# Output columns 1024 to 2047 with a fourth pair by seven products, and written orders for the sums, the passage and the end

## The chip, the cores and the metric

The kernel runs on one core of one Trainium2 chip. The metric is the device time in microseconds of one execution. A core has TensorE (PE in the profile, with PEld for its loads of weights), VectorE (DVE), ScalarE (ACT), GpSimd (POOL) and SyncE (SP), which issues nearly all transfers here. Each engine takes its own queue of instructions in order and waits at an instruction until what it needs is there.

## The reference

One layer of a gated short convolution with modulation by a vector c, for 256 tokens, D = 2048 and E = 4096:

```python
h = rmsnorm(x, norm_g)
mod = silu(c) @ ada_w + ada_b
shift, scale, gate = split(mod, 3)
h = h * (1 + scale) + shift
b_gate, c_gate, v, g = split(h @ w_in, 4)          # 2048 -> 4 * 4096
u = causal_depthwise_conv(c_gate * v, conv_w)      # width 3
y = b_gate * u * silu(g)
out = rmsnorm(x + gate * (y @ w_out), final_g)     # 4096 -> 2048
```

All is float32. The kernel splits each float32 factor of the large products into a rounded high part and a low part, and adds three products: high by high, low by high, high by low.

## The kernel before

**Up to the output product.** The input product (L491) and all that stands ahead of it fill the first 727 us; the diff leaves them as they are but for one instruction on ACT near their end. The result y lies as 16 pairs of row blocks (`ys[0]` to `ys[15]`, each 256 rows of E by 256 tokens, in high and low parts).

**The output product** runs in two halves of 1024 output columns, both by `columns`. Each step n takes one pair j from a written order: it loads 256 rows of `w_out` by 1024 columns (1 MB, `load_o`, L711), ACT makes the high part by a cast (`split_hi`, L352), DVE the low part by a subtraction (`split_lo`, L357), and PE multiplies (`triple`, L722): for 2 tiles of 128 tokens, 2 row blocks and 2 groups of 512 columns, 3 matmuls each, so 24 matmuls of 512 columns.

Pairs in `sevens` go through `seven` instead: a 2 by 2 block product by seven products in place of eight, with sums of blocks of y (`forms`, made earlier for pairs 10 to 15) and of the weights. That is 21 matmuls. DVE makes the sums of the weights (L742, L744, L745) and the low part of the weights as they are (1536 wide, L746), ACT their high part (1536 wide, L743), and then the sums are split like a normal pair's piece (2048 wide, L352 and L357). When the last of the `sevens` is through, `gather` (L764, L765) brings their shared sums into `ends`.

**Buffers.** Loaded weights and sums of weights take turns in three buffers of the kind "lo"; a load is issued once DVE has done with the piece that lay there three turns before. High parts take turns in three buffers of the kind "hi", low parts in three of "raw"; these come free when PE is through with the piece of three turns before.

**The passage between the halves.** When the first half is done, DVE adds its banks to `ends`, applies the gate, adds x and weights by `final_g` (`gated`, L730 to L733), and ACT takes the squares, while PE runs the first pairs of the second half.

**The end.** Columns 1024 to 1535 (the third quarter) and 1536 to 2047 (the fourth) end apart. In the second half's `columns` the fourth quarter gets pairs 0 to 5 and 10 to 15, and so does the third. The pieces of `LAST` (ep 3 and 4, pairs 6 to 9) then come for the third quarter alone. The fourth quarter's sums so far are gated, x is added (L847 to L849), and ACT copies them into the banks `po[0]` and `po[1]` (L850), one per tile of tokens t. The weights of the last pieces are multiplied by the gate on DVE (L862), split, and PE adds them straight onto `po[t]`: 24 matmuls for t = 0, 24 for t = 1. The root of the norm (L818, which needs ACT's table of roots), the scaling (`finish`, L824 to L828) and the stores (L829) close each t.

**What sets the order.** A scheduler places each engine's instructions by a simulated timeline; `tc.add_manual_dep` with `after` keeps one instruction behind another on its engine without any signal, `in_order` does so for all instructions of a block, and `later` lowers a block's priority.

Of the kernel before, what the change touches and what calls it, by code (L numbers as in the profile page):

```python
# [13 lines left out]
P = 128  # L14
D = 2048
# [102 lines left out]
def short_conv_layer(ctx: ExitStack, tc: tile.TileContext, x, c, norm_g, ada_w, ada_b, w_in, conv_w, w_out, final_g, out):  # L118
# [224 lines left out]

    def hi_tile():
        return w_tile("hi", "hi", F32R)
# [9 lines left out]
    def split_lo(raw, n, hi, lo_tag="lo", lo=None):  # L355
        lo = lo_tile(lo_tag) if lo is None else lo
        nc.vector.tensor_tensor(out=lo[:, :n], in0=raw[:, :n], in1=hi[:, :n].bitcast(F32), op=ALU.subtract)  # L357
        return hi, lo
# [271 lines left out]
    forms = {}  # L630

# [22 lines left out]
    for ct in range(NS, NCT, 2):  # L654
        for q in QUARTERS:
# [25 lines left out]
            elif q == 3:  # L681
                nc.scalar.activation(z, bank, AF.Silu)
# [23 lines left out]

    fsq = const.tile([P, TT, 3], F32, tag="fsq", name="fsq")
# [16 lines left out]
    def gated(t, c0, n, src, pr, at):  # L724


        cs = slice(c0, c0 + n)
        r = xr[:, t, cs]
        g = gates[c0 // 1024].rearrange("p a f -> p (a f)")[:, c0 % 1024 : c0 % 1024 + n]
        nc.vector.tensor_tensor(out=pr, in0=src, in1=g, op=ALU.mult)  # L730
        nc.vector.tensor_tensor(out=r, in0=r, in1=pr, op=ALU.add)
        nc.scalar.activation(pr, r, AF.Square, scale=D**-0.5, accum_out=fsq[:, t, at : at + 1])
        nc.vector.tensor_tensor(out=r, in0=r, in1=fg[:, cs], op=ALU.mult)  # L733


    def seven(j, raw, bank, p1, p6, p75, opens, last):
# [5 lines left out]
        nc.vector.tensor_tensor(out=s[:, 0:2], in0=b[:, 1:3], in1=b[:, 0:1].to_broadcast([P, 2, W]), op=ALU.subtract)  # L742
# [67 lines left out]
    for t in range(TT):  # L810
        c = ends[t].rearrange("p h f -> p (h f)")
        with later(350):
            gated(t, 0, 2 * W, c, c, 0)

    def finish(t):
# [20 lines left out]
        2 * W, (0, 1, 2, 10, 3, 13, 11, 4, 14, 12, 5, 15), SEVEN[0:3],  # L836
# [8 lines left out]
    for t in range(TT):  # L845
        c = ends[t][:, 1]
        nc.vector.tensor_tensor(out=c, in0=halves[1][:, t], in1=c, op=ALU.add)  # L847
        nc.vector.tensor_tensor(out=c, in0=c, in1=gate(3), op=ALU.mult)
        nc.vector.tensor_tensor(out=c, in0=c, in1=xr[:, t, 3 * W : 4 * W], op=ALU.add)  # L849
        nc.scalar.copy(po[t], c)  # L850
# [6 lines left out]
    late = []  # L857
    for ep in LAST:
# [4 lines left out]
        hi, lo = split(raw, SLOT, "raw")  # L863
        out_mm(po[0], 0, ep, hi, lo)
        late.append((ep, hi, lo))
    for t in range(TT):
        c = ends[t][:, 0]
        nc.vector.tensor_tensor(out=c, in0=halves[0][:, t], in1=c, op=ALU.add)
        gated(t, 2 * W, W, c, c, 1)
# [3 lines left out]
    for t in range(TT):  # L873
        if t == 1:
            for ep, hi, lo in late:
                out_mm(po[1], 1, ep, hi, lo)
        nc.scalar.activation(ends[t][:, 1], po[t], AF.Square, scale=D**-0.5, accum_out=fsq[:, t, 2:3])
        finish(t)
# [24 lines left out]
```

## Time and profile before

| | us |
|---|---|
| median of 3 runs (lowest, highest) | 905.64 (905.23, 906.0) |
| the profiled execution's own time | 905.34 |
| its span, first to last instruction | 903.6 |
| PE, output product begins | 726.73 |
| PE, second half begins | 809.92 |
| DMA, mean share of its 16 engines in the last 24 us | 0.25 |

The page gives for each engine its busy time; a timeline row gives start, length, engine, line, what is written from what, and in brackets how long the engine stood idle ahead of it and what released it. A matmul's length in the timeline is longer than the distance to the next, since matmuls overlap. In a row of chain or waits "PE mm L722 <- ACT mm L850" reads: the matmuls of line 722 into an `mm_1` bank waited for ACT's write into it at line 850. The two banks named `mm_1` serve the sevens as `p1` and `p6` and afterwards as `po[0]` and `po[1]`.

### The profile page before, as it was taken

To read this page: it belongs to the slowest core of one execution; us is meant where nothing else is said; L and a number is where in the kernel's file an instruction comes from. 1 tells how busy PE (TensorE), PEld (TensorE's weight loads), DVE (VectorE), ACT (ScalarE), POOL (GpSimd) and SP (SyncE) were. 2 spreads that over 40 slices of the span, in tenths; PEclk is the share of its full clock that TensorE was granted. 3 is DMA by queue.
4 is the path that set the end of the run, shared out by engine and by line. 5 is a ranking of instruction groups with operands and counts; after the bars stand their busy time and mean duration, and the time that the engine had idled before them with its cause. 6 is when DMAs were issued, how large, how long until landed. Compare 5 with 4: busy or idle time off the path is not lost.

```text
span 903.6 us, 16403 instructions
## 1 busy us (share of the span) xinstructions
PE 888.2 (98%) x7000; PEld 851.0 (94%) x7000; DVE 670.2 (74%) x661; ACT 482.4 (53%) x427; POOL 87.3 (10%) x95
## 2 busy tenths in 40 slices
PE   7999999999999999999999999999999999999996
PEld 4899999999999999999999999999999988888884
DVE  5889989888888867765875677565555578889685
ACT  6767866665548756644433434443434435544443
POOL 0000000000000132024324303320000000000000
PEclk9999999999999999999999999999999999999999
DMA  9999999999998587687988888866666486675652
GB/s 309 366 368 368 363 313 354 353 369 351 351 328 286 162 279 247 187 257 236 287 238 241 257 279 263 248 211 200 188 187 190 138 304 209 212 251 163 214 182 94
DMA packets 159594, 235.01 MB, mean 260 GB/s; under 512 B 6804, under 2 KB 105284, under 8 KB 159136
## 3 DMA queue, kind: packets, MB, share of 16 engines
q1 hardware_dynamic: 156384, 226.56, 76.7%
q0 software_dynamic: 3008, 7.34, 2.8%
q8 instruction: 55, 0.90, 0.4%
q14 instruction: 19, 0.16, 0.1%
q10 hardware_dynamic: 128, 0.04, 0.0%
HBM read 224.49 MB, written 2.10 MB: 251 GB/s over the span
## 4 chain that ended last, share of the span: by engine, by line
PE 90%; DMA 4%; DVE 2%; ACT 1%; SPq 1%; issue 1%; ACTq 0%
PE mm_b L491 39%; PE mm_s L491 36%; PE mm_w L722 7%; PE mm_o L722 5%; PE mm L722 4%; DMA at<-in_ada_w_dram 2%; DVE lo L357 1%; SPq L231 1%; DMA raw_s<-in_sc_w_in_dram 1%; ACT hi L352 1%; DMA x<-in_x_dram 1%; DMA raw_o<-in_sc_w_out_dram 1%; PE tp_g L481 0%; DVE raw_o L862 0%; ACT mm_s L524 0%
## 5 line engine op out<-in xcount | busy, mean ns | idle before, releaser
L491 PE MATMUL mm_s<-hT,hi 128*128 128x256 f32 x2048 | 350.3, 277 | 1.8 <-ACT hT L328 1.0
L491 PE MATMUL mm_b<-hT,hi 128*128 128x256 f32 x2048 | 348.2, 276 | 0.0
L491 PEld LDWEIGHTS mm_s<-hT,hi 128*128 128x128 f32 x2048 | 308.1, 188 | 2.4 <-ACT hT L328 1.2
L491 PEld LDWEIGHTS mm_b<-hT,hi 128*128 128x128 f32 x2048 | 308.6, 188 | 0.0
L491 PE MATMUL mm_b<-hT,lo 128*128 128x256 f32 x1024 | 282.6, 276 | 0.0
L491 PE MATMUL mm_s<-hT,lo 128*128 128x256 f32 x1024 | 282.0, 277 | 0.1
L357 DVE TENSOR_TENSOR lo<-raw,hi 128x2048 fp32r<-128x2048 f32 (+1 forms) x66 | 151.8, 2301 | 101.4 <-ACT hi L352 101.1
L352 ACT CAST hi<-raw 128x2048 fp32r<-128x2048 f32 (+1 forms) x66 | 123.7, 1875 | 191.6 <-PE mm_b L491 150.7
L491 PEld LDWEIGHTS mm_b<-hT,lo 128*128 128x128 f32 x1024 | 192.2, 188 | 0.0
L491 PEld LDWEIGHTS mm_s<-hT,lo 128*128 128x128 f32 x1024 | 191.7, 188 | 0.3 <-DVE lo L357 0.3
L357 DVE TENSOR_TENSOR lo<-raw_s,hi 128x2048 fp32r<-128x2048 f32 (+1 forms) x80 | 149.3, 1872 | 39.6 <-ACT hi L352 39.1
L352 ACT CAST hi<-raw_s 128x2048 fp32r<-128x2048 f32 (+1 forms) x80 | 123.9, 1557 | 56.1 <-PE mm_s L491 51.7
L474 DVE SCALAR_TENSOR_TENSOR gv<-at,silu_c,gv 128x512 f32<-128x512 f32 x105 | 78.6, 749 | 3.6 <-DMA at<-in_ada_w_dram 1.9
L512 ACT COPY acc<-mm_s 128x1024 f32<-128x1024 f32 x54 | 54.7, 1013 | 42.4 <-PE mm_s L491 42.3
L357 DVE TENSOR_TENSOR lo<-raw_o,hi 128x2048 fp32r<-128x2048 f32 x23 | 52.5, 2289 | 25.7 <-ACT hi L352 25.7
L352 ACT CAST hi<-raw_o 128x2048 fp32r<-128x2048 f32 x23 | 43.8, 1908 | 48.4 <-PE mm_o L722 17.3
L722 PE MATMUL mm_o<-hi,y 128*128 128x512 f32 x188 | 59.0, 389 | 0.0
L722 PE MATMUL mm_w<-hi,y 128*128 128x512 f32 x184 | 58.8, 389 | 0.0
L623 POOL TENSOR_TENSOR gacc<-gacc,z 128x512 f32<-128x512 f32 x28 | 45.9, 1639 | 119.3 <-DMA z<-gacc 119.3
L617 DVE SCALAR_TENSOR_TENSOR gacc<-at_g,silu_c,gacc 128x512 f32<-128x512 f32 x60 | 45.9, 764 | 8.0 <-DMA at_g<-in_ada_w_dram 6.9
L621 POOL DMA_DIRECT2D z<-gacc x28 | 15.7, 561 | 330.6 <-DVE acc L558 284.9
L722 PEld LDWEIGHTS mm_o<-hi,y 128*128 128x128 f32 x188 | 35.3, 188 | 7.3
(152 smaller groups left out, 675.4 us busy)
## 6 DMA issues: line engine op xcount, KB each, us to landing
raw<-in_sc_w_in_dram SPq DMA_DIRECT2D x64, 1024.0 KB, 5.8
raw_s<-in_sc_w_in_dram SPq DMA_DIRECT2D x47, 1024.0 KB, 7.7
raw_o<-in_sc_w_out_dram SPq DMA_DIRECT2D x32, 1024.0 KB, 5.2
at<-in_ada_w_dram SPq DMA_DIRECT2D x114, 256.0 KB, 7.8
raw_s<-in_sc_w_in_dram SPq DMA_DIRECT2D x33, 512.0 KB, 6.7
at_g<-in_ada_w_dram SPq DMA_DIRECT2D x32, 512.0 KB, 7.8
at<-in_ada_w_dram SPq DMA_DIRECT2D x6, 512.0 KB, 9.3
x<-in_x_dram SPq DMA_DIRECT2D x4, 512.0 KB, 6.2
```

Of the source, the lines that this page charges most:

```text
L231: nc.sync.dma_start(at[:, :, s, :], adas[:, j : j + kk, s, 0 : NK0 * P])
L352: nc.scalar.copy(hi[:, :n], raw[:, :n])
L357: nc.vector.tensor_tensor(out=lo[:, :n], in0=raw[:, :n], in1=hi[:, :n].bitcast(F32), op=ALU.subtract)
L474: nc.vector.scalar_tensor_tensor(out=gv, in0=at4[:, i], scalar=c_k, in1=gv, op0=ALU.mult, op1=ALU.add)
L491: mm = last_mm[0] = nc.tensor.matmul(dst, w, h[k], start=begins and left, stop=ends, skip_group_check=True)
L512: nc.scalar.copy(acc[ch, q], bank)
L617: nc.vector.scalar_tensor_tensor(out=ga, in0=at3[:, i, :], scalar=s, in1=ga, op0=ALU.mult, op1=ALU.add)
L621: nc.gpsimd.dma_start(turned[0 : P - away], ga[away:P])
L623: nc.gpsimd.tensor_tensor(out=ga, in0=ga, in1=turned, op=ALU.add)
L722: nc.tensor.matmul(dst, y[a], b, start=opens and i == 0, stop=ends and i == 2, skip_group_check=True)
```

## The change

- The second half's order of pairs becomes 0, 1, 2, 10, 3, 11, 4, 12, 5, 13, 14, 15, and its `sevens` are 10 to 13 in place of 10 to 12.
- In `seven` the first sum of the weights stays behind the last low part that was traced before it.
- `gated` is divided into `residual` and `weighted`; its operations stay the same.
- The passage of the fourth quarter into `po` (`move`), the gate product of the last pieces (`gated_piece`) and everything behind them stand in one `in_order` block: piece 3, then the three sums and the copy of t = 0, then piece 4, then those of t = 1; `finish(0)` is traced ahead of `po[1]`'s matmuls, and t = 1's third quarter is weighted behind `finish(0)`.
- A root of a constant (`warm2`) is taken behind the last SiLU, so that ACT's table of roots is loaded there.

```diff
+    last_silu = ended_silu[0]
+    warm2 = const.tile([P, 1], F32, tag="fs", name="warm2", bufs=2)
+    early = nc.scalar.activation(warm2, eps_t, AF.Sqrt)
+    tc.add_manual_dep(early.ins, last_silu.ins.name, after, reason="the table of roots is there at the end")
...
-        nc.vector.tensor_tensor(out=s[:, 0:2], in0=b[:, 1:3], in1=b[:, 0:1].to_broadcast([P, 2, W]), op=ALU.subtract)
+        first = nc.vector.tensor_tensor(
+            out=s[:, 0:2], in0=b[:, 1:3], in1=b[:, 0:1].to_broadcast([P, 2, W]), op=ALU.subtract
+        )
+        if last_low[0] is not None:
+            tc.add_manual_dep(first.ins, last_low[0].ins.name, after, reason="the pair in front comes first")
...
-        2 * W, (0, 1, 2, 10, 3, 13, 11, 4, 14, 12, 5, 15), SEVEN[0:3],
+        2 * W, (0, 1, 2, 10, 3, 11, 4, 12, 5, 13, 14, 15), SEVEN[0:4],
...
+    with in_order():
+        late = []
+        for t, ep in enumerate(LAST):
+            raw = gated_piece(ep)
+            hi = split_hi(raw, SLOT)
+            move(t)
+            late.append((ep, *split_lo(raw, SLOT, hi, "raw")))
+        for ep, hi, lo in late:
+            out_mm(po[0], 0, ep, hi, lo)
+        third(0)
+        third_weighted(0)
+        third(1)
+        for t in range(TT):
+            nc.scalar.activation(ends[t][:, 1], po[t], AF.Square, scale=D**-0.5, accum_out=fsq[:, t, 2:3])
+            finish(t)
+            if t == 0:
+                third_weighted(1)
+                for ep, hi, lo in late:
+                    out_mm(po[1], 1, ep, hi, lo)
```

`move(t)` holds the three sums and the copy of before (L847 to L850), `gated_piece` the load and the gate product (L862), `third` and `third_weighted` what stood at L868 to L872.

**On PE, second half.** A row is line, operation, output from inputs. `mm_1` is the bank `p1` of the sevens, `mm_o` the two wide banks, y12 a block of pair 12. Before, at the start of pair 14, which follows the normal pair 4:

```order
L722 MATMUL mm_o_8866<-hi_9092,y4_4136 128x512
L722 MATMUL mm_o_8866<-lo_9094,y4_4136 128x512
L722 MATMUL mm_o_8866<-hi_9092,y4_4136 128x512
L722 MATMUL mm_o_8865<-hi_9122,y14_4466 128x512
L722 MATMUL mm_o_8866<-hi_9122,y14_4466 128x512
L722 MATMUL mm_1_8868<-hi_9153,y12_4464 128x512
L722 MATMUL mm_o_8865<-lo_9124,y14_4466 128x512
L722 MATMUL mm_o_8865<-hi_9122,y14_4466 128x512
L722 MATMUL mm_o_8866<-lo_9124,y14_4466 128x512
```

Now, at the start of pair 4, which follows the seven products of pair 11:

```order
L731 MATMUL mm_1_8871<-hi_9037,form_6501 128x512
L731 MATMUL mm_o_8868<-lo_9039,y11_4463 128x512
L731 MATMUL mm_o_8868<-hi_9037,y11_4463 128x512
L731 MATMUL mm_o_8867<-hi_9064,y4_4136 128x512
L731 MATMUL mm_o_8868<-hi_9064,y4_4136 128x512
L731 MATMUL mm_1_8870<-hi_9095,y12_4464 128x512
L731 MATMUL mm_o_8867<-lo_9066,y4_4136 128x512
L731 MATMUL mm_o_8867<-hi_9064,y4_4136 128x512
L731 MATMUL mm_o_8868<-lo_9066,y4_4136 128x512
```

Pair 12's first matmul stands third in the normal pair ahead of it in both; that pair was the second of two and is now the only one between two sevens. Pair 11's stands in the same way in pair 3.

**On DVE, passage between the halves.** `mm_w` are the first half's banks, `z0` and `z1` are `ends` of t = 0 and 1, `big` holds x and the sums. Before, from the first half's last sums to the low part of pair 10:

```order
L809 TENSOR_TENSOR z0_4470<-mm_w_8333,z0_4470 128x1024
L742 TENSOR_TENSOR sums_o_8962<-raw_o_8960 128x1024
L809 TENSOR_TENSOR z1_4471<-mm_w_8334,z1_4471 128x1024
L730 TENSOR_TENSOR z0_4470<-z0_4470,gate0_4468 128x1024
L744 TENSOR_TENSOR sums_o_8962<-raw_o_8960,sums_o_8962 128x512
L357 TENSOR_TENSOR lo_8934<-raw_o_8930,hi_8932 128x2048
L730 TENSOR_TENSOR z1_4471<-z1_4471,gate0_4468 128x1024
L731 TENSOR_TENSOR big_8329<-big_8329,z0_4470 128x1024
L745 TENSOR_TENSOR sums_o_8962<-raw_o_8960,sums_o_8962 128x512
L731 TENSOR_TENSOR big_8329<-big_8329,z1_4471 128x1024
L746 TENSOR_TENSOR lo_8964<-raw_o_8960,hi_8963 128x1536
```

Now, the same stretch:

```order
L825 TENSOR_TENSOR z0_4470<-mm_w_8335,z0_4470 128x1024
L825 TENSOR_TENSOR z1_4471<-mm_w_8336,z1_4471 128x1024
L738 TENSOR_TENSOR z0_4470<-z0_4470,gate0_4468 128x1024
L738 TENSOR_TENSOR z1_4471<-z1_4471,gate0_4468 128x1024
L359 TENSOR_TENSOR lo_8936<-raw_o_8932,hi_8934 128x2048
L754 TENSOR_TENSOR sums_o_8964<-raw_o_8962 128x1024
L739 TENSOR_TENSOR big_8329<-big_8329,z0_4470 128x1024
L739 TENSOR_TENSOR big_8329<-big_8329,z1_4471 128x1024
L760 TENSOR_TENSOR sums_o_8964<-raw_o_8962,sums_o_8964 128x512
L746 TENSOR_TENSOR big_8329<-big_8329 128x1024
L761 TENSOR_TENSOR sums_o_8964<-raw_o_8962,sums_o_8964 128x512
L762 TENSOR_TENSOR lo_8966<-raw_o_8962,hi_8965 128x1536
```

The first sum of pair 10's weights now follows pair 2's low part, and one weighting by `final_g` (`big<-big`) has come ahead of pair 10's low part.

**On DVE, the end.** `gate1` is the gate of the upper half, `raw_o` by `gate1` the gate product of a last piece. Before:

```order
L862 TENSOR_TENSOR raw_o_9318<-raw_o_9318,gate1_4469 128x2048
L357 TENSOR_TENSOR lo_9292<-raw_o_9288,hi_9290 128x2048
L862 TENSOR_TENSOR raw_o_9337<-raw_o_9337,gate1_4469 128x2048
L847 TENSOR_TENSOR z0_4470<-mm_o_8866,z0_4470 128x512
L847 TENSOR_TENSOR z1_4471<-mm_o_8866,z1_4471 128x512
L357 TENSOR_TENSOR lo_9323<-raw_o_9318,hi_9321 128x2048
L848 TENSOR_TENSOR z0_4470<-z0_4470,gate1_4469 128x512
L848 TENSOR_TENSOR z1_4471<-z1_4471,gate1_4469 128x512
L357 TENSOR_TENSOR lo_9342<-raw_o_9337,hi_9340 128x2048
L849 TENSOR_TENSOR z0_4470<-z0_4470,big_8329 128x512
L849 TENSOR_TENSOR z1_4471<-z1_4471,big_8329 128x512
```

Now:

```order
L359 TENSOR_TENSOR lo_9291<-raw_o_9287,hi_9289 128x2048
L881 TENSOR_TENSOR raw_o_9317<-raw_o_9317,gate1_4469 128x2048
L872 TENSOR_TENSOR z0_4470<-mm_o_8868,z0_4470 128x512
L873 TENSOR_TENSOR z0_4470<-z0_4470,gate1_4469 128x512
L874 TENSOR_TENSOR z0_4470<-z0_4470,big_8329 128x512
L359 TENSOR_TENSOR lo_9326<-raw_o_9317,hi_9320 128x2048
L881 TENSOR_TENSOR raw_o_9328<-raw_o_9328,gate1_4469 128x2048
L872 TENSOR_TENSOR z1_4471<-mm_o_8868,z1_4471 128x512
L873 TENSOR_TENSOR z1_4471<-z1_4471,gate1_4469 128x512
L874 TENSOR_TENSOR z1_4471<-z1_4471,big_8329 128x512
L359 TENSOR_TENSOR lo_9337<-raw_o_9328,hi_9331 128x2048
```

The three sums of t = 0 stand together ahead of the first last piece's low part, those of t = 1 ahead of the second's. Ahead of these rows, pair 15's low part now follows three of the four sums of the gathering, where it followed one.

51 lines of the change are left out of this document (25 added, 26 removed).

## The prediction

> **What bounds the kernel now.** I read the page first, for the share of each engine.
>
> ```profile
> span 903.6 us, 16403 instructions
> PE 888.2 (98%) x7000; PEld 851.0 (94%) x7000; DVE 670.2 (74%) x661; ACT 482.4 (53%) x427; POOL 87.3 (10%) x95
> ```
>
> TensorE (PE) is busy 98% of the span, so an edit pays only if it takes matmuls away or closes a hole between them. The diff touches nothing before the output product, so the second view is PE's waits from 735 us to the end; it has one row. The third is the chain of waits round that hole, with columns start, length, what.
>
> ```profile
> PE mm L722 <- ACT mm L850: 0.8, 1, 0.8
> ...
> 846.18 6.35 PE mm_o L722 x28
> ...
> 874.45 2.29 DVE raw_o L862
> 876.74 1.20 DVE z L847 x2
> 877.93 2.20 DVE lo L357
> 880.13 1.21 DVE z L848 x2
> 881.34 2.20 DVE lo L357
> 883.54 0.61 DVE z L849
> 884.15 0.02 issue
> 884.18 0.60 ACT mm L850
> 884.78 0.04 issue
> 884.82 11.23 PE mm L722 x48
> 896.05 0.02 issue
> 896.07 0.70 ACT z L877 x2
> ```
>
> Twenty-eight matmuls in 6.35 us are 0.2268 us each, without a hole. The only hole stands ahead of the last 48: they need the bank `po[0]`, which ScalarE (ACT) fills at L850 from sums that VectorE (DVE) makes at L847 to L849, and DVE has two gate products and two low parts queued among those sums. What lies behind the last matmul, 896.07 to 903.6, is t=1's square, root, scaling and stores. The fourth view is the timeline of PE round the hole, start and length first.
>
> ```profile
> 883.65 0.39 PE L722 MATMUL mm_o<-hi,y 128*128 128x512 f32 x1
> 884.82 0.50 PE L722 MATMUL mm<-hi,y 128*128 128x512 f32 x1 [0.79 <-ACT mm L850]
> 885.16 0.40 PE L722 MATMUL mm<-lo,y 128*128 128x512 f32 x1
> ...
> 895.65 0.39 PE L722 MATMUL mm<-hi,y 128*128 128x512 f32 x1
> ```
>
> From the start at 883.65 to that at 895.65 are 12.00 us; 48 matmuls at 0.2268 are 10.88. The hole costs **1.12 us**: 0.94 of lateness and the rest in slow first matmuls behind it.
>
> **The change, part by part.** *Seven products for pair 13.* A normal pair is 24 matmuls, a pair by seven products 21. Three are gone: 3 × 0.2268 = **0.68 us**, as long as PE stays the bound here. DVE and ACT pay for it: the sums and a second pair of parts. In the first 1024 columns sevens and normal pairs already alternate, as 10 to 13 now do in the second, and PE's waits show nothing there; that work is hidden by the matmuls of the pair in front. One thing differs. In the second half the scheduler puts the first matmul of pairs 11 and 12 third in the normal pair ahead of them, and PE takes its queue in order. Before, two normal pairs lay between sevens and there was time; now one does. So I follow pair 12's high part from a cycle of the first half, and then from the rows where the second half begins.
>
> ```profile
> 750.01 2.29 DVE L357 TENSOR_TENSOR lo<-raw_o,hi 128x2048 fp32r<-128x2048 f32 x1 [0.98 <-ACT hi L352]
> 756.59 0.37 SPq L711 DMA_DIRECT2D raw_o<-in_sc_w_out_dram  x1
> 761.73 1.48 ACT L743 CAST hi<-raw_o 128x1536 fp32r<-128x1536 f32 x1 [1.55 <-DMA raw_o<-in_sc_w_out_dram]
> ...
> 828.26 4.49 DVE L357 TENSOR_TENSOR lo<-raw_o,hi 128x2048 fp32r<-128x2048 f32 x2 [2.00 <-ACT hi L352]
> 830.61 0.84 PE L722 MATMUL mm_o<-hi,y 128*128 128x512 f32 x3
> DMA to landing us min/median/max: 5.0/5.2/6.7
> ```
>
> From the low part of a normal pair to the next load is 6.58 us (the seven in between must let go of its buffer), to the cast of what that load brought 11.72. Pair 3's low part stands at 828.26 and keeps its place, so pair 12's cast starts at 839.98 and ends at 841.46; its matmul can start 0.04 later, the step that the chain shows behind L850: 841.50. PE would get to it after pair 3 (whose first matmul is the second of the three at 830.61: 830.84), pair 11 and two more, 24 + 21 + 2 = 47 matmuls: 841.50. Nothing is to spare. A wait also costs the slow restart, 1.12 - 0.94 = 0.18. Bounds: nothing if the load is a hair early; if it takes the 6.7 us that is the longest here, instead of 761.73 - 756.59 = 5.14, then 1.56 + 0.18 = 1.74. I take **0.15 us**, near the median landing of 5.2.
>
> The Trainium skill, page "DMA: Bandwidth & Descriptors", section "Anatomy of one DMA — SWDGE (gpsimd) path", fits a transfer as 2.0 us plus its bytes at 436 GB/s, for that path; for 1024 KB that is an estimate of 4.4 us, and the wait would be nil. By that rule the whole gain of 1.80 us would come; the trace does not agree, its shortest landing is 5.0.
>
> Pair 11's matmul is placed in the same way in pair 3, at 830.84 + 2 × 0.2268 = 831.29. Its buffer comes free at the end of pair 10's low part, which the new order at the seam puts behind one more operation on the first 1024 columns, a weighting by L733.
>
> ```profile
> 806.46 2.29 DVE L357 TENSOR_TENSOR lo<-raw_o,hi 128x2048 fp32r<-128x2048 f32 x1 [3.15 <-ACT hi L352]
> 821.68 1.22 DVE L733 TENSOR_TENSOR big<-big 128x1024 f32<-128x1024 f32 x1
> ```
>
> DVE is without a pause from 806.46 on, and that low part ended at 821.7, where L733 starts. Now L733's 1.2 us and a short wait for the square in front of it come first, so about 823.2; plus 5.2 of landing and 1.48 of cast is 829.9, 1.4 us early. This costs nothing unless the load takes over 6.6 us.
>
> *Order of passage and end.* Now each gate product is followed by one t's three sums, and then the low part. By the chain's durations: gate 2.2, three dependent sums 3 × 0.65 (0.61 and the step between), low part 2.2, and the same again, 12.7 us. When does it start?
>
> ```profile
> 862.57 2.28 DVE L357 TENSOR_TENSOR lo<-raw_o,hi 128x2048 fp32r<-128x2048 f32 x1
> 865.97 2.28 DVE L357 TENSOR_TENSOR lo<-raw_o,hi 128x2048 fp32r<-128x2048 f32 x1
> 870.04 2.29 DVE L862 TENSOR_TENSOR raw_o<-raw_o,gate 128x2048 f32<-128x2048 f32 x1 [1.19 <-DMA raw_o<-in_sc_w_out_dram]
> ```
>
> The load for the gate product waits for pair 15's low part (862.57 + 2.28, then 5.14 to 870.04). That low part now stands behind two more sums of the gathering, 1.2 us, with everything 0.68 earlier: the data are there at 870.6. The low parts of both pieces of LAST now stand in front of it as well, the second where the third quarter's cast lets it; I start the gate at 871.3. Then `po[0]`'s sums end at 871.3 + 2.2 + 1.95 = 875.5, ACT's copy at 876.1; PE asks for it at 883.87 - 0.68 = 883.2. The second low part ends at 884.0; PE asks for it after 12 matmuls of the first, at 886.1 with the leading one. The hole is closed with 7 us to spare at the copy and **2.1 us** at the low part, so the gain is the whole **1.12 us**. If that cover goes, each us of slip beyond 2.1 costs one.
>
> Behind it, t=0's third quarter (DVE 884.0 to about 887.4) and t=1's three sums (to 889.4) run under the 24 matmuls of `po[0]`, which end at 888.8; t=1's square and weighting run under the 24 of `po[1]`, to about 893 against 894.2. The tail of 7.56 us behind the last matmul keeps its instructions: 0.
>
> *Early root.* The table that t=0's root needs is loaded today under `po[1]`'s matmuls, so moving it gains nothing at the end.
>
> ```profile
> 717.79 0.58 ACT L682 ACTIVATE z<-mm_b 128x512 f32<-128x512 f32 x1
> 721.37 1.91 ACT L352 CAST hi<-raw_o 128x2048 fp32r<-128x2048 f32 x1 [3.00 <-PE mm_b L491]
> 891.40 1.28 ACT L818 ACT_TABLE_LOAD   x1
> 892.70 0.30 ACT L818 ACTIVATE fs<-fsq,part_sum 128x1 f32<-128x1 f32 x1
> ```
>
> It moves to 718.4, where ACT has 3.00 us idle until PE frees a buffer; 1.28 + 0.30 fit. It costs 0, and 1.6 at most if that idle time were gone.
>
> **Sum.** -0.68 - 1.12 + 0.15 = -1.65 us: the span goes from 903.6 to 901.95. The profiled execution took 905.34, 1.74 beyond its span, so 903.69 by its own time. It lies 0.30 under the median of the three runs, 905.64; against that median the forecast is **904.0 us**, -0.18%.
>
> **Rivals.** *A, the whole gain.* Pair 12's load is early and nothing waits: -1.80 us, 903.8. For it: landings go down to 5.0, and the cycle above is only even. Against: even is the best the rows give, and any lateness brings the restart with it.
>
> *B, the early-placed matmuls eat the gain.* With landings of 5.7 to 6.7 pair 12 waits 0.7 to 1.74 and pair 11 up to 0.3: 904.5 to 905.9. For it: 6.7 did occur in this half. Against: the median is 5.2, and only two loads count.
>
> *C, slower.* The same place, with loads as slow as where the DMA engines are fuller.
>
> ```profile
> raw_s<-in_sc_w_in_dram SPq DMA_DIRECT2D x47, 1024.0 KB, 7.7
> raw_o<-in_sc_w_out_dram SPq DMA_DIRECT2D x32, 1024.0 KB, 5.2
> ```
>
> At 7.7 pair 12 waits 2.56 + 0.18 and pair 11 (823.2 + 7.7 + 1.5 = 832.4 against 831.29) 1.1 + 0.18: 4.0 us, which leaves +2.2 and 907.8. It decides from landings of about 6.5, where the two waits reach 1.8. Against it stands the second row. The end could add to it, past its 2.1 us.
>
> *D, that the change does not do what it says:* if the hole only moves, say to the copy of `po[1]`, 0.68 remain, 905.0. The order gives that copy 884.0 - 2.2 + 0.6 = 882.4 against 888.6, so I count this within B.
>
> **How the numbers follow.** Forecast 0.52, A 0.28, B with D 0.11, C 0.09. A measurement of this kernel tells some 0.2% (1.81 us) from no change; the full gain of 1.80 lies just there. The three runs spread 0.77 us, so of A's share I count 0.6 as faster by over 0.2%, of the forecast's 0.35, as its small wait is put between nothing and a few tenths: 0.17 + 0.18 = 0.35. Slower by over 0.2% takes C's upper part and what no row told me, 0.10; 0.55 remain within. The range begins where A falls with a low run, 903.84 - 0.64, and takes in most of B: 903.2 to 905.7.
>
> **What would show it.** Right: 3 matmuls fewer; no wait of PE on the copy into `po[0]`; L733's successors under the last 48 matmuls; the table load near 718; the last matmul some 1.65 us earlier, the tail at 7.5 to 7.6. In pair 4 of the second half, third matmul, a wait of PE on the 1536-wide cast of 0 to 0.4 us: over 0.7 is B, none is A. Wrong: a new wait on a low part in the last 24 us, a tail longer by over 0.3, or a wait of PE elsewhere in the second half.

## The result

| | before | changed kernel |
|---|---|---|
| median of 22 runs each | 905.51 us | 904.18 us |
| lowest to highest | 904.59 to 906.00 | 903.40 to 904.77 |
| span of the profiled execution | 903.6 us | 902.2 us |
| matmuls | 7000 | 6997 |

The ratio is 0.9986, with a 95% interval of 0.9979 to 0.9992. The kernel is 1.33 us faster, and its median lies 0.18 us from the forecast of 904.0. Part of that nearness is luck: the forecast was counted from the median of three runs, 905.64; from the median of 22, 905.51, the same sum would have given 903.86, 0.32 us too low. The gain of 0.14% is under the 0.2% that the prediction set as what a measurement of this kernel can tell; with 22 runs of each kernel the interval lies wholly below 1.

To compare executions below I use one length: from the start of the first matmul into `mm_o` in the second half (the beginning of what the change touches) to the start of the last matmul of all. Where it starts differs between executions by up to 1 us (the 809.92 given above for the kernel before is the end of the first half's last matmul). The length was 809.75 to 895.65, **85.90 us**, before, and is 809.69 to 894.14, **84.45 us**, now: 1.45 less. What follows the last matmul's start, the tail, was 7.95 and is 8.06. Two traces of the same kernel can differ: a second one of the change has a length of 84.58 and a tail of 8.35.

**The page of the changed kernel**, its first lines:

```profile
span 902.2 us, 16405 instructions
PE 887.1 (98%) x6997; PEld 850.1 (94%) x6997; DVE 676.2 (75%) x665; ACT 484.5 (54%) x429; POOL 88.0 (10%) x95
```

Three matmuls fewer, four operations more on VectorE and two on ScalarE. The view of waits of the same stretch as in the prediction, from 735 us to the end, is empty now for PE; its loads of weights (PEld) have two rows, of which this is the first:

```profile
PEld mm L731 <- ACT hi L759: 0.5, 1, 0.5
```

The row that names the copy into `po[0]` is gone, and this one is at the place that the prediction named: the matmul of pair 12 that stands third in pair 4's queue, waiting for the cast of 1536 elements (L759 now). PE's timeline there, and at the end:

```profile
840.75 0.84 PE L731 MATMUL mm_o<-hi,y 128*128 128x512 f32 x3
841.65 0.50 PE L731 MATMUL mm<-hi,y 128*128 128x512 f32 x1
841.99 0.40 PE L731 MATMUL mm_o<-lo,y 128*128 128x512 f32 x1
...
894.14 0.39 PE L731 MATMUL mm<-hi,y 128*128 128x512 f32 x1
```

Three matmuls from 840.75 on, 0.2268 apart, would let the next one start at 841.43. It starts at 841.65, 0.22 late, and the one behind it 0.34 later instead of 0.23, another 0.11: **0.33 us** are lost. The chain of waits shows what came last ahead of it, and then the end of the kernel:

```profile
834.77 5.26 DMA raw_o<-in_sc_w_out_dram
...
840.12 1.49 ACT hi L759
...
841.65 0.50 PE mm L731
...
861.44 22.21 PE mm_o L731 x98
883.65 10.89 PE mm L731 x48
```

Before, the last 48 matmuls started 0.94 us late, behind work of VectorE and ScalarE, and took 11.23 with their slow start. Now 98 and 48 matmuls follow each other at 0.2268 each: the hole is closed. VectorE's timeline shows by how much it is ahead at the end:

```profile
872.04 2.29 DVE L881 TENSOR_TENSOR raw_o<-raw_o,gate 128x2048 f32<-128x2048 f32 x1
...
882.92 2.29 DVE L359 TENSOR_TENSOR lo<-raw_o,hi 128x2048 fp32r<-128x2048 f32 x1
```

The gate product starts at 872.04 and the second low part ends at 885.2 (it was put at 871.3 and 884.0). PE asks for that part 13 matmuls behind the first of the 48, whose record stands at 883.49: 886.4. 1.2 us are left of the 2.1.

### The profile page after: what moved, and what is told of

It is laid out like the page before. It is cut to its first block, busy times and chain, and to the rows that moved or that the text cites. A ratio compares the mean times of both kernels' runs of the same rounds, so it can differ in the third digit from the quotient of the medians.

```text
span 902.2 us, 16405 instructions
## 1 busy us (share of the span) xinstructions
PE 887.1 (98%) x6997; PEld 850.1 (94%) x6997; DVE 676.2 (75%) x665; ACT 484.5 (54%) x429; POOL 88.0 (10%) x95
## 4 chain that ended last, share of the span: by engine, by line
PE 92%; DMA 4%; ACT 1%; SPq 1%; DVE 1%; issue 1%; ACTq 0%
PE mm_b L495 39%; PE mm_s L495 36%; PE mm_w L731 7%; PE mm_o L731 6%; PE mm L731 4%; DMA at<-in_ada_w_dram 2%; DMA raw_s<-in_sc_w_in_dram 1%; SPq L231 1%; ACT hi L354 1%; DMA raw_o<-in_sc_w_out_dram 1%; DMA x<-in_x_dram 1%; PE tp_g L485 0%; ACT mm_s L528 0%; ACT acc L516 0%; DVE lo L762 0%
## 5 line engine op out<-in xcount | busy, mean ns | idle before, releaser
L359 DVE TENSOR_TENSOR lo<-raw_o,hi 128x2048 fp32r<-128x2048 f32 x22 | 50.4, 2291 | 23.4 <-ACT hi L354 23.4
L627 POOL TENSOR_TENSOR gacc<-gacc,z 128x512 f32<-128x512 f32 x28 | 48.3, 1726 | 109.0 <-DMA z<-gacc 109.0
L731 PE MATMUL mm_o<-hi,y 128*128 128x512 f32 x176 | 55.3, 389 | 0.0
L731 PEld LDWEIGHTS mm_w<-hi,y 128*128 128x128 f32 x184 | 34.5, 188 | 7.1
```

Source lines behind the costliest of these rows:

```text
L359: last_low[0] = nc.vector.tensor_tensor(out=lo[:, :n], in0=raw[:, :n], in1=hi[:, :n].bitcast(F32), op=ALU.subtract)
L627: nc.gpsimd.tensor_tensor(out=ga, in0=ga, in1=turned, op=ALU.add)
L731: nc.tensor.matmul(dst, y[a], b, start=opens and i == 0, stop=ends and i == 2, skip_group_check=True)
```

## The experiments

The lengths, tails and medians together; start and last matmul are rows of PE's timeline in each trace. Where the median is of one run, the kernel was run once, for its trace. The kernel before had medians of 905.33 to 905.56 beside them.

| kernel | second half starts | last matmul | length | tail | median | ratio (95%) |
|---|---|---|---|---|---|---|
| before | 809.75 | 895.65 | 85.90 | 7.95 | 905.51 | |
| the change | 809.69 | 894.14 | 84.45 | 8.06 | 904.18 | 0.9986 (0.9979 to 0.9992) |
| three sevens, new end | 809.83 | 894.60 | 84.77 | 7.90 | 904.18 | 0.9985 (0.9976 to 0.9993) |
| three sevens, old end | 809.67 | 895.76 | 86.09 | 7.94 | 905.46 (one) | |
| four sevens, old end | 809.13 | 893.68 | 84.55 | 8.92 | 904.53 | 0.9993 (0.9984 to 1.0001) |
| no early root | 809.09 | 893.76 | 84.67 | 8.34 | 904.12 | 0.9984 (0.9976 to 0.9993) |
| sums not held | 809.94 | 897.75 | 87.81 | 8.35 | 905.61 | 1.0007 (0.9998 to 1.0015) |
| sums not held, again | 810.14 | 896.85 | 86.71 | 8.05 | 906.72 (one) | |
| first matmul held | 809.67 | 894.43 | 84.76 | 8.27 | 904.00 | 0.9988 (0.9979 to 0.9996) |
| cast in two | 809.37 | 893.47 | 84.10 | 8.13 | 903.86 | 0.9985 (0.9976 to 0.9994) |
| cast in two, again | 809.83 | 893.97 | 84.14 | 8.43 | 904.21 | 0.9987 (0.9978 to 0.9996) |
| the change, again | 809.77 | 894.35 | 84.58 | 8.35 | 904.27 | 0.9988 (0.9979 to 0.9997) |
| five sevens | 810.02 | 895.47 | 85.45 | 8.33 | 905.55 | 1.0003 (0.9994 to 1.0012) |
| five sevens, room made | 809.63 | 894.59 | 84.96 | 10.11 | 906.09 | 1.0005 (0.9996 to 1.0014) |

The medians from 903.86 to 904.53 agree with one another within their intervals; among these kernels only the traces, one execution each, tell a few tenths apart. Two traces of one kernel differ by 0.13 in length (the change) and by 0.04 (the cast in two), and by 0.3 in the tail.

The tails hold something that the prediction left out. With three sevens they are 7.90 to 7.95, with four and the new end 8.05 to 8.43. In the three traces with three sevens the second of t = 1's stores is issued 2.62 to 2.63 us behind the last matmul's start, the last one at 3.59; in every trace with four sevens it is 2.94 to 2.95 and 3.86 to 3.88. The early root and the end have no share in this, since it stays without either. Why a fourth seven delays these stores by 0.3 us the traces don't show.

### Which part closes the hole

*Three sevens with the new end.* The change, with the order of pairs and the three sevens of before.

```diff
-        2 * W, (0, 1, 2, 10, 3, 11, 4, 12, 5, 13, 14, 15), SEVEN[0:4],
+        2 * W, (0, 1, 2, 10, 3, 13, 11, 4, 14, 12, 5, 15), SEVEN[0:3],
```

> The second half's old order of pairs with three sevens; sums, end and root as in the change. Theory (the span moves by PE's matmuls and its holes alone: three matmuls 0.68 us, the hole ahead of po[0] 1.12, the early-placed matmul in pair 4 minus 0.35): no hole at the end and none in the second half, since two normal pairs lie between the sevens again; last matmul 1.1 us earlier than before, span 902.4 to 902.6, ratio to before 0.9988. Rival (the hole closes because the fourth seven shifts DVE's work, not by the written order): a hole of 0.5 to 1 us ahead of po[0] stays, span 903.0 to 903.6.

Measured: 84.77, and no wait of PE from 735 us on. From 85.90 that is -1.13, the predicted 1.12, without the fourth seven. Its median is that of the change, 904.18: the fourth seven takes away three matmuls and shows no gain in time, since the wait in pair 4 and the longer tail together take back 0.49 in the first trace of the change (0.33 + 0.16) and 0.92 in the second (0.47 + 0.45).

*Three sevens with the old end.* The same, and the end traced as before the change (the sums' rule and the early root stay).

```diff
-    with in_order():
-        late = []
-        for t, ep in enumerate(LAST):
-            raw = gated_piece(ep)
...
+    for t in range(TT):
+        if t == 1:
+            for ep, hi, lo in late:
+                out_mm(po[1], 1, ep, hi, lo)
```

> Three sevens in the old order and the end as before, with the change's sums and early root. Theory (with three sevens the scheduler's end makes the hole, and only the written order closes it there; sums and root move nothing): the hole ahead of po[0] is back as in the kernel before, 1.1 us of PE's time from the second half's start to the last matmul against the run with the written end, 85.9 us. Rival (the hole was closed by the order of sums or the root): no hole, 84.8 us.

The hole is back. PE's one wait of this kernel, and the chain in front of it:

```profile
PE mm L731 <- ACT mm L867: 1.0, 1, 1.0
```

```profile
881.46 2.20 DVE lo L359
883.66 0.61 DVE z L866
...
884.29 0.60 ACT mm L867
```

The last sum for `po[0]` (L866) stands behind the second low part, as it did in the kernel before. So with three sevens the written order of the end closes the hole; the sums' rule and the root, which this kernel has as well, don't close it.

*Four sevens with the old end.* The change, with only its end undone, by the same edit.

> The change with the end as before (scheduler's order, no written block); fourth seven, sums and root stay. Theory as put in the prediction (the written order closes the hole): the hole ahead of po[0] is back with 0.5 to 1.1 us, last matmul 0.3 to 0.4 us earlier than before, span 903.2 to 903.4, ratio 0.9996. Rival (the scheduler, given another stretch in front, places t = 0's sums ahead of the second low part by itself): no hole, but the matmuls of po[0] and po[1] are mixed and t = 0 ends only 12 matmuls ahead of t = 1, whose square then waits up to 0.3 us for ACT: last matmul as in the change, span 902.2 to 902.6.

I had expected the hole to come back here as well. It does not: the length is 84.55, and PE waits nowhere but at pair 12's cast. VectorE's timeline shows why:

```profile
878.00 2.28 DVE L359 TENSOR_TENSOR lo<-raw_o,hi 128x2048 fp32r<-128x2048 f32 x1
880.20 1.28 DVE L866 TENSOR_TENSOR z<-z,big 128x512 f32<-128x512 f32 x2
881.41 2.28 DVE L359 TENSOR_TENSOR lo<-raw_o,hi 128x2048 fp32r<-128x2048 f32 x1
```

With four sevens the scheduler puts the last sums at 880.20, ahead of the second low part, by itself. What the old end costs here lies in the tail: 8.92 against 8.06. ScalarE's timelines, first of this kernel and then of the change, where L845 is the scaling of t = 0 that its stores need:

```profile
891.44 0.60 ACT L895 ACTIVATE z<-mm 128x512 f32<-128x512 f32 x1 [3.38 <-PE mm L731]
892.69 1.34 ACT L845 ACTIVATE big<-big,fs 128x512 f32<-128x512 f32 x2 [0.23 <-DVE fs L836]
```

```profile
889.19 0.60 ACT L908 ACTIVATE z<-mm 128x512 f32<-128x512 f32 x1 [1.17 <-PE mm L731]
891.16 1.34 ACT L845 ACTIVATE big<-big,fs 128x512 f32<-128x512 f32 x2 [0.96 <-DVE fs L836]
```

The scheduler mixes the matmuls of `po[0]` and `po[1]`, so `po[0]` is done 2.25 us later (its square starts at 891.44 against 889.19), though this execution's second half began 0.56 earlier and its last matmul comes 0.46 earlier. The transfers from 889 to 907 us, in 40 slices of 0.45 us, with the share of the DMA engines in tenths, show what follows. First this kernel, then the change:

```profile
DMA  0000000000079999999998168000000000000000
```

```profile
DMA  0000000099999920008899995000000000000000
```

In the change t = 0's stores are through before t = 1's begin; with the old end they begin some 1.35 us later and run into them. The last store takes 3.9 us to land, where it takes 3.0 and 3.3 in the two traces of the change, and the kernel ends 0.4 us later although PE ended earlier. So the written end is worth 1.3 us with three sevens (86.09 - 84.77) and 0.5 to 0.9 us, in another place, with four (a tail of 8.92 against 8.06 to 8.43 in the traces with the new end). The medians, 904.53 against 904.18 and 904.27, don't tell these kernels apart.

### The early root

```diff
-    early = nc.scalar.activation(warm2, eps_t, AF.Sqrt)
-    tc.add_manual_dep(early.ins, last_silu.ins.name, after, reason="the table of roots is there at the end")
```

> The change without the early root; the table is loaded ahead of t = 0's root. Theory (the early root is worth nothing here): t = 0's root 1.28 us later, all of it under po[1]'s matmuls; the last matmul and the tail behind it as in the change to 0.1 us, span 902.1 to 902.3, ratio 0.9986. Rival (the written order of ACT and DVE behind t = 0's root leaves less room than that, since t = 1's third quarter is squared and summed behind finish(0)): the tail grows by 0.2 to 0.5 us, span 902.4 to 902.7.

Measured: 84.67, with the matmul behind pair 12's cast 0.43 late, where it is 0.22 late in the change, and 904.12 us. The tail of 8.34 is 0.28 above the change's 8.06, within the rival's 0.2 to 0.5; but the change itself has 8.35 in its second trace, with the root, so the root does not account for it. ScalarE's timeline of the changed kernel, and of the one without the root:

```profile
718.24 1.28 ACT L714 ACT_TABLE_LOAD   x1
719.53 0.20 ACT L714 ACTIVATE warm<-eps_t 128x1 f32<-128x1 f32 x1
721.20 1.91 ACT L354 CAST hi<-raw_o 128x2048 fp32r<-128x2048 f32 x1 [1.47 <-PE mm_b L495]
```

```profile
889.51 1.28 ACT L831 ACT_TABLE_LOAD   x1
```

At 718 the load and the root fit in idle time with 1.47 us to spare; at 889.51 the load lies under the matmuls of `po[1]`, which end past 893. It costs nothing measurable at either place, as predicted.

### The wait in pair 4

*First matmul held.* The first matmul of a seven stays behind the pair in front.

```diff
+            if held and i == 0:
+                tc.add_manual_dep(mm.ins, last_out[0].ins.name, after, reason="behind the pair in front")
```

> The change, with the first matmul of each seven held behind the last matmul of the pair in front of it on PE. Theory (0.35 us are lost where pair 12's first matmul, third in pair 4's queue, waits for its cast): no wait and no slow restart in pair 4, the last matmul 0.35 us earlier than in the change, span 901.8 to 901.9, ratio 0.9982. Rival (pair 12's weights are simply late, and the wait only moves to pair 12's own start): last matmul as in the change, span 902.2, a wait of 0.2 us or more at pair 12.

Neither came: the wait on the cast is gone, and the length is 84.76. The chain of waits:

```profile
830.49 7.05 DMA raw_o<-in_sc_w_out_dram
...
837.64 1.91 ACT hi L354
...
841.92 4.17 PE mm_o L733 x17
```

In this execution pair 4's own load took 7.05 us, where it took 5.5 in the change, and PE lost 0.62 us (0.52 and 0.10 of slow restart) on pair 4's low part instead. The edit is not the reason for the slow load: in the second execution of the change the same load takes 7.12 us. So this kernel doesn't answer what the held matmul is worth.

*Cast in two.* The order stays, but the block that the early matmul needs is cast first, on its own.

```diff
-        nc.scalar.copy(bh[:, 1:4], b[:, 1:4])
+        nc.scalar.copy(bh[:, 1:2], b[:, 1:2])
+        nc.scalar.copy(bh[:, 2:4], b[:, 2:4])
```

> The change with the 1536-wide cast of each seven as two casts, the 512 columns that the early-placed matmul needs first. Theory (the wait in pair 4 ends with that cast): ready 0.8 us earlier, no wait there, second half to last matmul 84.1 us against 84.45; the scheduler then places pairs 12 to 15 of the first half and 13 of the second early too, which must not wait, since there the loads land as early. Rival (the wait is for the load, which can also be over 0.8 us later than in that execution): waits remain at one or more of those places, 84.3 us or more.

ScalarE's and then PE's timeline of this kernel:

```profile
839.53 0.62 ACT L759 CAST hi<-raw_o 128x512 fp32r<-128x512 f32 x1 [1.26 <-DMA raw_o<-in_sc_w_out_dram]
```

```profile
840.43 0.84 PE L731 MATMUL mm_o<-hi,y 128*128 128x512 f32 x3
841.11 0.39 PE L731 MATMUL mm<-hi,y 128*128 128x512 f32 x1
```

The matmul comes 0.68 behind the start of the three, on its beat, and PE and PEld wait nowhere from 735 us on. The length is 84.10: 0.35 less than the change and 1.80 less than before, the whole of 0.68 + 1.12. But the division need not be the reason. The load took 5.0 us here and 5.3 in the changed kernel, and even an undivided cast, 1.48 us from 839.53, would have ended at 841.01, ahead of PE's 841.11. So both kernels were run again, side by side.

> The change with the cast of 1536 divided, again. In its first look pair 12's load took 5.08 us, 0.18 less than in the changed kernel, and with that even an undivided cast (1.48 us from 839.53) would have ended 0.06 us before PE's 841.11, so that look doesn't tell what the division does. Theory (the first block's cast is all that the early matmul needs, so a load of up to some 6 us brings no wait): no wait of PE at pair 4's third matmul whatever the load takes, here too where landing and 1.48 us of cast would be late, and 84.1 us from the second half's first matmul to the last one's start. Rival (the division did nothing, the early load did): with a load of 5.2 us or more a late start of 0.2 to 0.4 there, and 84.4 to 84.7.

> The changed kernel beside the one with the cast in two, on the same chip. Theory (its wait comes with every load of 5.2 us or more): a late start of 0.2 to 0.4 at pair 4's third matmul, 84.4 to 84.7 us from the second half's first matmul to the last one's start, and a median 0.2 to 0.5 us above that of the kernel with the cast in two. Rival (the wait is an accident of some executions): no late start, 84.1, and equal medians.

The chain of the changed kernel's second execution, and ScalarE's and PE's timelines of the divided one's:

```profile
834.85 5.39 DMA raw_o<-in_sc_w_out_dram
...
840.34 1.49 ACT hi L759
841.83 0.04 issue
841.87 0.50 PE mm L731
```

```profile
840.07 0.62 ACT L759 CAST hi<-raw_o 128x512 fp32r<-128x512 f32 x1 [1.10 <-DMA raw_o<-in_sc_w_out_dram]
```

```profile
840.88 0.84 PE L731 MATMUL mm_o<-hi,y 128*128 128x512 f32 x3
841.56 0.39 PE L731 MATMUL mm<-hi,y 128*128 128x512 f32 x1
```

The change waits again (0.36 late and 0.11 of restart, 84.58), and the divided cast again doesn't (84.14). In this execution of the change the division could have saved little: pair 4's own load took 7.12 us, so pair 4's low part, which the matmul behind needs, was done at 842.04 (839.75 + 2.29), and that matmul started at 842.21 as it was. With the cast divided the first block was ready at 840.69, 0.9 us ahead of PE; undivided it would have ended at 841.55, and 0.04 more makes 841.59 against 841.56: even. The load took 5.1 us this time, below the 5.2 of the expectation, so the trial with a late load did not come about. What stands is that in four executions with this order and an undivided cast (the change twice, the old end, no early root) the load took 5.3 to 5.5 us and PE started 0.22 to 0.43 late, and in two with the divided one it took 5.0 to 5.1 and PE did not wait. Whether the division itself brings the earlier landing is open. In the medians side by side, 904.21 and 904.27, the 0.4 us don't show. The kernel with the cast in two has the shortest length of all, and its times don't set it apart from the change.

### The sums behind the pair in front

```diff
-        if last_low[0] is not None:
-            tc.add_manual_dep(first.ins, last_low[0].ins.name, after, reason="the pair in front comes first")
```

> The change without the rule that a seven's first sum stays behind the last low part in front of it. Theory (the rule buys nothing by itself; in a normal pair the low part then comes 1.2 us later, behind the first sum, and the next load 1.2 us later): pair 4's low part at 839.8 instead of 838.6 still meets its matmul at 841.9, so only the early-placed matmul waits, by 0.2 to 0.5 us; the scheduler places pair 13's first matmul early as well, in pair 5, with another such wait of 0.2 to 0.5 us. Second half to last matmul 84.5 to 85.0 us (84.45 in the change). Rival (the rule is what keeps normal pairs on time): waits of PE on low parts of pairs 3, 4 or 5 of over 0.5 us in all, 85.0 us or more.

The theory fell and the rival held: 87.81, 3.36 more than the change. VectorE's timeline of this kernel:

```profile
840.42 1.22 DVE L754 TENSOR_TENSOR sums_o<-raw_o 128x1024 f32<-128x1024 f32 x1 [4.00 <-DMA raw_o<-in_sc_w_out_dram]
841.56 2.28 DVE L359 TENSOR_TENSOR lo<-raw_o,hi 128x2048 fp32r<-128x2048 f32 x1
```

and ScalarE's at the same place:

```profile
837.80 1.91 ACT L354 CAST hi<-raw_o 128x2048 fp32r<-128x2048 f32 x1 [3.71 <-DMA raw_o<-in_sc_w_out_dram]
```

Pair 4's high part is there at 839.7, but in VectorE's queue the sums of pair 12 stand first and wait for pair 12's load until 840.42, VectorE idle for 4.00 us in front of them, and pair 4's low part starts at 841.56, 1.85 us later than it could. PE's timeline shows the wait, and that what follows runs slowly:

```profile
843.90 0.69 PE L731 MATMUL mm_o<-lo,y 128*128 128x512 f32 x1 [1.44 <-DVE lo L359]
...
845.24 1.05 PE L731 MATMUL mm_o<-hi,y 128*128 128x512 f32 x2
846.09 0.63 PE L731 MATMUL mm_o<-lo,y 128*128 128x512 f32 x1
```

The table of windows says by which clock: start and end, length, five busy times with their counts, then the granted clock of PE, the share of the DMA engines, GB/s.

```profile
843.90:847.40 3.50, 3.50 (x9) 2.73 (x10) 3.09 (x4) 1.91 (x1) 0.00 (x0) 0.52 0.66 204
```

Late starts of 0.27 and 1.72 us, and 1.7 us more in matmuls that stand 0.43 apart instead of 0.2268. Did the slow stretch come of the wait? A second execution of the same kernel was to tell; its window row stands behind the expectation.

> The change without the rule that holds a seven's sums behind the pair in front, a second look. The first look had two waits of 0.27 and 1.72 us in pair 4 and behind them 3.5 us at a granted clock of 0.52, 87.81 us in all; its times lay only 1.4 us above the change's. Theory (the slow stretch follows from the wait): again a wait of over 1 us at pair 4, and behind it a stretch of some 3.5 us with a clock near 0.5. Rival (the slow stretch was that execution's own): the same waits with a clock of 1.00 behind them, and 86.0 to 86.5 us from the second half's first matmul to the last one's start.

```profile
844.60:848.10 3.50, 3.49 (x15) 2.93 (x16) 3.08 (x4) 1.92 (x1) 0.00 (x0) 1.00 0.67 179
```

The waits are there again (0.8 late at 842.67, 1.71 at 844.61, 0.11 of restart: 2.62 in all, and 84.10 + 2.62 = 86.72 against the measured 86.71), but the clock behind them stays at 1.00. So such waits don't always bring a slow stretch. Whether it was an accident is less sure: of the eleven runs of this kernel three took 907.79 to 907.88 us, the traced one (907.83) among them, and the other eight 904.48 to 905.74. Of the two other long ones there is no trace.

Not all of this is the order of the queue: pair 4's own load took some 7 us in both executions. The change with the rule had such a load as well, in its second execution, as ScalarE's timeline shows; pair 4's cast starts at the same time as in the first trace without the rule:

```profile
837.82 1.91 ACT L354 CAST hi<-raw_o 128x2048 fp32r<-128x2048 f32 x1 [2.64 <-DMA raw_o<-in_sc_w_out_dram]
```

There it cost 0.47 us in all (84.58), and 0.62 in the kernel with the first matmul held; here the late starts come to 2.0 to 2.5. So with nearly equal loads of pair 4 (7.04 and 7.12 us) the rule is worth about 2.1 us (86.71 - 84.58). By the medians, whose runs need not all have such a load, it is 1.4 us, and the whole gain of the change is gone without it: 1.0007. The rule matters with the fourth seven: with three sevens and the old end, the kernel that has it (86.09, 905.46) and the kernel before, without it (85.90, 905.51), are alike.

### A fifth seven

Pair 14 by seven products as well, with the first matmuls held as above.

```diff
-        2 * W, (0, 1, 2, 10, 3, 11, 4, 12, 5, 13, 14, 15), SEVEN[0:4],
+        2 * W, (0, 1, 10, 2, 11, 3, 12, 4, 13, 5, 14, 15), SEVEN[0:5],
```

> Five sevens in the second half, in the order of the first half's alternation (0, 1, 10, 2, 11, 3, 12, 4, 13, 5, 14, 15), each seven's first matmul held behind the pair in front. Theory (each seven is worth three matmuls, 0.68 us, while DVE keeps up): second half to last matmul 84.45 - 0.35 - 0.68 = 83.4 us, less what DVE loses where the passage of the first half now meets pair 10's sums one pair earlier (0 to 0.8 us); span 901.1 to 902. Rival (DVE is at its limit with alternate sevens, so that the passage's 9 us push every low part back): waits of PE on low parts of 1 us or more, 84.4 us or more, span 902.2 or more.

The rival held: 85.45, 1.0 us more than the change. PE's waits of this kernel:

```profile
PE mm_o L733 <- DVE lo L359: 0.9, 1, 0.9
PE mm L733 <- DVE lo L359: 0.5, 1, 0.5
```

Two holes of 1.17 and 0.82 with their restarts, at pair 2's low part (behind the two weightings by `final_g`) and at the second low part of the end. 84.10 - 0.68 + 1.99 = 85.41. Then room was made at just these places: the weightings behind the low parts of pairs 3 and 4, and both gate products ahead of both low parts. In the edit `by_final` is the last line of `weighted`, now a function of its own, and `lows` lists the low parts in the order in which they are traced.

```diff
+        mult = by_final(t, 0, 2 * W)
+        tc.add_manual_dep(mult.ins, lows[second + 5 + 2 * t].ins.name, after, reason="off the seam")
...
+        raws = [gated_piece(ep) for ep in LAST]
+        his = [split_hi(raws[0], SLOT)]
+        move(0)
+        his.append(split_hi(raws[1], SLOT))
+        late = [(ep, *split_lo(raw, SLOT, hi, "raw")) for ep, raw, hi in zip(LAST, raws, his)]
+        move(1)
```

> Five sevens in the second 1024 columns, as in the kernel with five before it, with room made where that one's two waits stood: the two weightings of the first 1024 columns by final_g (L751 there, 1.2 us each on VectorE) no longer stand ahead of pair 2's low part but behind those of pairs 3 and 4, and at the end both gate products come ahead of both low parts, with t=1's three sums behind these. Theory (a seven is worth its 3 matmuls, 0.68 us, wherever VectorE has its parts ready; five sevens lost 0.9 + 0.5 us only by these two places in VectorE's queue): no wait above 0.2 us at pair 2 and at the end's second low part, and from the second half's first matmul to the last one's start 84.10 - 0.68 = 83.4 to 83.7 us, a span of 901.0 to 901.5. Rival (VectorE has no room left for 5 sevens: what is taken from one place is late at the next): a wait of PE on a low part of pair 3, 4 or 5, or on the end's, of 0.5 us or more, and 84.2 or longer.

```profile
PE mm_o L735 <- ACT hi L355: 0.5, 1, 0.5
PE mm_o L735 <- DVE lo L360: 0.3, 1, 0.3
```

The wait at the end is gone, but pair 2 still waits and another normal pair now waits for its cast at 865.35. Pair 2's low part shows what is late there now, on ScalarE's timeline:

```profile
820.89 1.05 ACT L752 ACTIVATE z<-big 128x1024 f32<-128x1024 f32 x1
...
821.93 1.89 ACT L355 CAST hi<-raw_o 128x2048 fp32r<-128x2048 f32 x1
```

The square of t = 1's first 1024 columns stands ahead of its cast, and the cast follows as soon as it is done. VectorE itself stands idle for 1.59 us ahead of that low part, and the cast at 863.39 that the other wait is for stood 1.62 us behind PE, so neither wait shows VectorE to be full, as the rival had it. And t = 1's sums, moved behind both low parts, push the third quarter back, so that t = 1's square starts at 896.33, 1.7 us behind the last matmul's start, and the tail grows to 10.11. Here what is taken from one place is late at the next: with five sevens neither of two orders paid. Whether a third would is open.

## Why the prediction was right

By its own steps:

- **Three matmuls, -0.68.** Held. From three sevens to four, both with the new end, is 84.77 to 84.45, -0.32, and that is -0.68 + 0.33 of wait; with the cast in two, where nothing waits, the difference is 84.77 - 84.10 = 0.67. This is PE's time. In the kernel's time it doesn't show: by the medians three sevens with the new end are as fast (904.18), and the fourth seven pays only for its own wait and its longer tail. Nor do the gains add up as the sum has them: either part closes the hole. From three sevens and the old end (905.46), the new end alone gives 904.18, the fourth seven alone 904.53, both 904.18.
- **The hole, -1.12.** Held in size: the end alone brought -1.13. The reason given, that the written order closes it, holds for three sevens. For four, the scheduler's own order had no hole either, and the written one earned 0.5 to 0.9 us in the tail, by letting t = 0's stores out before t = 1's. The prediction had read the order of the changed kernel alone, and never asked what the old end would become with the new order of pairs.
- **The early matmul of pair 12, +0.15.** Right place, right cause, and within the 0 to 0.4 us that the forecast named, but 0.33 in size (0.47 in the second execution). PE asked at 841.43, 0.07 sooner than the 841.50 of the sum, and the cast ended at 841.61, 0.15 later than the 841.46, as from the issue of its load to the cast were 5.35 us (834.77 to 840.12), not 5.14. To that come 0.11 of restart, where 0.18 was counted; the kernel before has 0.11 there too (885.16 - 884.82 against 0.2268).
- **Early root, 0.** Held: without the root the time is the same.
- **Tail, 0.** Not quite: 8.06 and 8.35 in the two traces of the change, against 7.95. The second is 0.40 longer, over the 0.3 that the prediction had named as a sign of being wrong. The term was put at nothing because the tail keeps its instructions; with four sevens its last stores are issued 0.3 us later.
- **Cover at the end.** 2.1 us were forecast, 1.2 are left: the gate product came 0.7 later than the 871.3 taken from the row of before.
- **The sums' rule.** Here the working was thin. The prediction counted the alternation of sevens and normal pairs as hidden work because the first half showed no wait, and gave the rule no term of its own. Without it the time goes back to 1.0007: with the fourth seven, the rule carries the gain of the whole change. In the sum the omission did no harm, since the changed kernel has the rule; but a reader would have taken it for an edit without weight.

The sum was -1.65, the length measured -1.45, the span -1.4, the medians -1.33. The 0.2 us between the first two are the wait's 0.18 and a few hundredths; the second trace of the change, with -1.32 in length and +0.40 in the tail, gained 0.9 us of span. The mechanism held; the wait and the tail were put too small.

**The rivals.** A, the whole gain, is what the length of the kernel with the cast in two shows (84.10), so its size was right; its condition, an early load, was met there and not in the changed kernel. B needed a wait of 0.7 or more, so a load of pair 12 of 5.7 us or more. In the seven traces with four sevens and the rule that load took 5.0 to 5.5 us; without the rule it took 6.55 and 6.85. It was pair 4's own load that went from 5.5 to 7.1 us in these seven, two of them of the same kernel, the change; the prediction didn't ask about that load, and why it varies stays open. C needed two slow loads at once, and no run of the change came near 907.8 (the highest of its 33 is 906.25). Of D, the copy of `po[1]` was never late.

By the Trainium skill, page "DMA: Bandwidth & Descriptors", section "Anatomy of one DMA — SWDGE (gpsimd) path", weighed in the prediction, the load of pair 12 would have taken an estimated 4.4 us and nothing would have waited. The trace does not agree: 5.26 us for that load, with a wait behind it.

## What to carry to other kernels

Where an engine takes its queue in order, ask of every operation that waits for a transfer what stands behind it: one sum placed ahead of a ready low part cost as much as all else in this change gained. When work is taken from the bound engine, what lies beside it has less cover; the fourth seven's three matmuls came back as a wait and a longer tail, and a fifth seven made the kernel slower than the change. And take two traces of a kernel before a few tenths are put down to an edit: a load that landed 0.3 us sooner was worth as much as the edit on trial.

## What was not expected of the hardware

In one execution PE ran for 3.5 us at a granted clock of 0.52 behind two late starts of 0.27 and 1.72 us; the same kernel, run again, had late starts of 0.8 and 1.71 us and a clock of 1.00 behind them. Late starts of 0.94, 1.15 and 1.07 us in three other traces (before; three sevens, old end; five sevens) were followed by no fall either. The slow stretch cost some 1.7 us in that one trace, so one trace alone would have put them down to the edit. Loads of the same 1 MB, issued at the same place in the second half, landed after 5.5 us in one execution of the changed kernel and after 7.1 in the other. By the Trainium skill, page "TensorE: Matmul & The Clock Gate", section "What's actually happening", the clock falls to half after an idle window of some 3.4 us; the two late starts in front of the slow stretch here sum to 2.0 us, so the trace shows a fall with less.
